# Two fused transformer blocks on one core: the second block opened with diagonal products and a channel-major first chunk

## The chip, the cores and the metric

One Trainium2 (trn2) chip, one of its cores. The metric is the device time of one execution of the whole program in microseconds (us), median of the runs shown; smaller is better. Engines are TensorE (PE in the profile; PEld is its weight load), VectorE (DVE), ScalarE (ACT), GpSimd (POOL) and SyncE (SP, which here only issues DMA transfers).

## What is computed

Batch 1, 512 tokens, width 1024, float32 in and out. The first block is attention plus a short convolution, then 16 experts of which each takes its 64 best tokens; the second block follows on its output.

```python
# end of block 1 (16 experts, 64 tokens each)
ye = (silu(xe @ w_gate) * (xe @ w_up)) @ w_down * gate     # per expert
x  = x + g2 * scatter_add(ye)                              # "combine"
x  = rmsnorm(x, final_norm_g)                              # output of block 1

# block 2
h = rmsnorm(x, norm_g)
u, v, za, ab, ab_gate, zb, g_a, g_b = split(h @ w_in + b_in)
y_a = gelu(u) * spatial_mix(layernorm(gelu(v))) * silu(za)
y_b = silu(groupnorm(conv31(ab * sigmoid(ab_gate)))) * silu(zb)
x = x + (sigmoid(g_a) * (y_a @ w_pa) + sigmoid(g_b) * (y_b @ w_pb)) @ w_out
x = x + sigmoid(rmsnorm(x, ple_norm_g) @ w_ple_gate) * (p @ w_ple)
out = rmsnorm(x, final_g)
```

The two normalisations at the seam meet on the same row: with a = 1/rms of block 1's output row before its gain, and e = the factor that both norms make together, the kernel works with one row `acc` (the sum after the last expert), the gain row `fng` (final_norm_g), and two numbers a row, `ae`.

## The kernel before, in words

Tokens lie in four tiles of 128 (`NT = 4`), channels in eight of 128 (`KT = 8`). Every large product of block 2 is made in three passes: both operands are split into a rounded part ("h") and a rest ("l"), and h*h, h*l and l*h are added up in PSUM (`mm3`). A weight chunk is 1024 x 256; `Weights.load` lets SP fetch it into a raw tile `wr` (two buffers), `Weights.steps` gives eight small steps per chunk that split it (ACT rounds into `wh`, L250; DVE subtracts into `wl`, L248), and the chunk that TensorE works on carries the steps of the next chunk along (`ahead`). The order on each engine is the order of the program's lines; nothing reorders it.

**Experts** (loop `for p in range(8)`, two experts a turn, on the two halves of TensorE's columns): `pair_gemm` with the gate weights into `pa_`, with the up weights into `pu`, with the down weights into `py`. Weights come as 1 MiB tiles `ew` through `eload`: each tile that has been used gives its buffer to the next tile in line. In turn p the sums of turn p-1 are put back to the tokens (`combine_half`, one-hot rows `GT` times `ybuf`, added to `acc` by DVE, L1261). The last turn (p = 7) loads its down weights in smaller pieces, column half n = 0 first, then n = 1, into one `py` tile of two banks; the four combines of half 0 stand in one place, before the third quarter of half 1.

**Gain rows.** `spread` makes a row in all 128 partitions out of a column: DVE writes the column on four diagonals (L900), TensorE multiplies with a matrix of ones (L903), ACT copies out (L904), twice a row. Turn 5 makes two rows so (`fng`, and `gg`, the product of both gains), turn 7 one (`b_in` of the v part).

**Opening of block 2.** The half-1 sum `ylast` is made by DVE (L1378); four combines (L1257) add it. For each token tile DVE multiplies by `gg` into `hr` (`h2_gain`, partly on POOL), ACT squares `acc` with a running sum (L1291), DVE weighs the squares with the squared gain (`x2_sums`, L1295), DVE and POOL make the two factors (`x2_stats`, L1453, L1454, and `power`, L179), ACT scales the row (L1465), TensorE turns it around in eight 128 x 128 transposes (`put_T`, L1427), ACT and DVE write `h2` as h and l (L1429, L1430). TensorE's first chunk is v chunk 0, token-major (`v_chunk(0)`): its four token tiles can start as soon as their own `h2` columns are there. After it stand `POOL` transfers and, on POOL, the multiplication of `acc` by `fng` (`xf_gain`, L1547); then four times a channel-major chunk for `ab_gate` and one for `ab`, and v chunks 1 to 3. From the first `ab` chunk on, DVE works off 31 convolution taps per channel tile in the background (L1593).

Of the kernel before, what the change touches and what calls it, by code (L numbers as in the profile page):

```python
# [62 lines left out]
def tile_two_blocks(ctx: ExitStack, tc: tile.TileContext, a, out):  # L63
# [373 lines left out]
    ci = [0]  # L437
# [458 lines left out]
    def spread(dst, cols_, tmp_):  # L896

        for n in range(2):
            d_ = tmp_()
            DVE.tensor_mul(d_.rearrange("p (a b) -> p a b", b=128), ident[:, None, :].to_broadcast([128, 4, 128]),  # L900
                           cols_[:, 4 * n:4 * n + 4, None].to_broadcast([128, 4, 128]))
            p_ = bank()
            PE.matmul(p_, one, d_, start=True, stop=True)  # L903
            ACT.activation(dst[:, n * 512:n * 512 + 512], p_, AF.Copy)  # L904

# [387 lines left out]
    def x2_sums(t, n):

        DVE.tensor_tensor_reduce(sqx[t], sqx[t], rows2[:, 0, half(n)], 1.0, sq4[:, t, 0, 1:2] if n else 0.0,  # L1295
                                 op0=OP.mult, op1=OP.add, accum_out=sq4[:, t, n, 1:2])

    for p in range(8):
# [60 lines left out]
        i0 += 16  # L1359
        ybuf[p] = big("yb", [2, D], F32R)  # L1360
        for n in range(2):
            for q, (k0, nk) in enumerate(lasts[n]):
                if n and q == 2:
                    x2_half(0, 0, tmp)
                    for t in range(NT):
                        if t < NT - 1:
                            x2_half(t + 1, 0, tmp)
                        x2_sums(t, 0)
                tiles = [etiles[i0 + e][0] for e in range(2)]
                i0 += 2  # L1370
# [25 lines left out]
    w2 = a["w_in_2"][0]  # L1396
    U0, V0, ZA0, AB0, AG0, ZB0, GA0, GB0 = (i * D for i in range(8))
    specs = [(w2, V0)]
    for j in range(4):
        specs += [(w2, AG0 + 256 * j), (w2, AB0 + 256 * j)]  # L1400
    specs += [(w2, V0 + 256 * j) for j in range(1, 4)]
    for j in range(4):
        specs += [(w2, U0 + 256 * j), (w2, ZA0 + 256 * j)]
    for j in range(4):
        specs += [(w2, GA0 + 256 * j), (a["w_pa_2"][0], 256 * j)]
    specs += [(w2, GB0 + 256 * j) for j in range(4)]
    specs += [(w2, ZB0 + 256 * j) for j in range(4)]
    specs += [(a["w_pb_2"][0], 256 * j) for j in range(4)]
    for n in ("w_out_2", "w_ple_gate_2"):
        specs += [(a[n][0], 256 * j) + (("mx",) if j % 2 else ()) for j in range(4)]  # L1410
    W = Weights(specs, {"mx": lambda sh: (big3("wxh", sh, F32R), big("wxl", sh, F32R))})
    ci[0] = 0
    lead[0] = 1
    W.load(1)
    gg = cst3[:, 0:D]
    cmat = identr
    strip = gp.tile([128, 128], F32R, name="strip", tag="post")
    rsel = strip[0:64, 96:104]
    bvb = rows2[:, 1]

    def put_T(dst, t, row):

        for n in range(2):
            p_ = bank("pT", (4, 128))
            for i in range(4):
                c = n * 512 + i * 128
                PE.transpose(p_[:, i], row[:, c:c + 128], ident)  # L1427
            ts = slice(t * 128, t * 128 + 128)
            ACT.activation(dst.h[n][:, :, ts], p_, AF.Copy)  # L1429
            DVE.tensor_sub(dst.l[n][:, :, ts], p_, dst.h[n][:, :, ts].bitcast(F32))  # L1430
# [26 lines left out]
    hrs = [big3("hr", [D]) for t in range(NT)]

    def h2_gain(t, n, eng=DVE):
        eng.tensor_tensor(hrs[t][:, half(n)], arow(t, half(n)), gg[:, half(n)], op=OP.mult)  # L1460

    def h2_row(t):
        for n in range(2):
            r = hrs[t][:, half(n)]
            ACT.activation(r, r, AF.Copy, scale=ae[:, t, 1:2])  # L1465

    def xf_row(t):
        ACT.activation(arow(t), arow(t), AF.Copy, scale=ae[:, t, 0:1])

    w0 = W.steps(0, lo_engine=POOL)  # L1470

    def w0_do(*js):
        for j in js:
            w0[j]()
# [446 lines left out]
```

## Time and profile before

| | |
|---|---|
| median of 3 runs | 1718.19 us (1715.05 to 1718.56) |
| the profiled execution, its own time | 1718.02 us |
| its span in the profile | 1716.3 us |
| TensorE busy | 1669.9 us, 97% of the span |
| DVE / ACT / POOL busy | 54% / 34% / 4% |

The profile is read from the outside in: the shares by engine say that TensorE is nearly always at work; the table by stretches says where it is not; the timeline of a stretch says what it waits for there. "Busy" counts an instruction's time at either clock, so the column PEclk, the granted share of TensorE's full clock (1.00 is 2.4 GHz, 0.50 is 1.2 GHz), is to be read beside it. A product on fp32 operands shows as two records.

### The profile page before, as it was taken

The page shows a single profiled execution, that of the slowest core. Times are in us where ns is not written, and L with a number is a line of the kernel's source. Part 1 is how long each engine was busy: PE and PEld are TensorE (multiplying, and loading weights), DVE is VectorE, ACT ScalarE, POOL GpSimd, SP SyncE. Part 2 cuts the span into 40 slices and gives each one's busy share as a digit, 9 for nine tenths or more (in the row PEclk, how much of TensorE's full clock was granted, in tenths as well). Part 3 has the DMA queues.
Part 4 walks back from the last instruction along what each step waited for, and adds up shares of the span by engine and source line. Part 5 has one row for each costly group of instructions (what it writes and reads, how often), then busy time and mean ns, then how long its engine had stood idle before and what let it go on. Part 6 is the DMA issues. An engine that isn't in the chain of part 4 may idle for free.

```text
span 1716.3 us, 22506 instructions
## 1 busy us (share of the span) xinstructions
PE 1669.9 (97%) x9212; PEld 1204.1 (70%) x9212; DVE 933.4 (54%) x1697; ACT 585.8 (34%) x1117; POOL 65.9 (4%) x68
## 2 busy tenths in 40 slices
PE   8999999989999999999999999979999999999998
PEld 5987787767888984444444344348898888877898
DVE  4667776565663442212121221286889999955544
ACT  5454444455222331111011011043335443354333
POOL 2000000000000000000000000050000000000000
PEclk9999999999999999999999999999999999999999
DMA  9132322202553769999999999833323233233421
GB/s 364 56 123 74 123 74 99 74 25 75 172 181 113 304 256 345 360 399 419 419 418 420 419 420 418 315 100 99 97 76 98 74 98 99 79 118 99 144 102 50
DMA packets 168028, 334.55 MB, mean 195 GB/s; under 512 B 6927, under 2 KB 103988, under 8 KB 167668
## 3 DMA queue, kind: packets, MB, share of 16 engines
q1 hardware_dynamic: 165520, 328.50, 51.6%
q0 software_dynamic: 1024, 2.37, 0.4%
q10 hardware_dynamic: 1380, 2.23, 0.4%
q8 instruction: 72, 1.18, 0.3%
q14 instruction: 32, 0.26, 0.0%
HBM read 328.89 MB, written 4.19 MB: 194 GB/s over the span
## 4 chain that ended last, share of the span: by engine, by line
PE 90%; DVE 6%; ACT 2%; issue 1%; DMA 1%; SPq 0%; POOL 0%; POOLq 0%; DVEq 0%; ACTq 0%
PE pb L289 16%; PE pb L290 15%; PE pb L291 15%; PE pu L1238 6%; PE py L1238 6%; PE pg L1202 4%; PE po L831 2%; PE pT L823 2%; PE s L792 1%; PE pg L1259 1%; PE pv L291 1%; PE py L1373 1%; PE pa__6640 L1238 1%; PE pa__6106 L1238 1%; PE pa__5837 L1238 1%
## 5 line engine op out<-in xcount | busy, mean ns | idle before, releaser
L248 DVE TENSOR_TENSOR wl<-wr,wh 128x512 fp32r<-128x512 f32 x316 | 225.2, 731 | 95.0 <-ACT wh L250 95.0
L250 ACT ACTIVATE wh<-wr 128x512 fp32r<-128x512 f32 x320 | 183.0, 620 | 78.8 <-PE pb L290 47.1
L1593 DVE SCALAR_TENSOR_TENSOR co<-cin,cols,co 128x512 f32<-128x512 f32 x240 | 188.3, 785 | 4.1
L289 PE MATMUL pb<-h2h,wh 128*128 128x512 f32 x448 | 177.4, 396 | 0.0
L290 PE MATMUL pb<-h2l,wh 128*128 128x512 f32 x448 | 174.9, 390 | 0.0
L291 PE MATMUL pb<-h2h,wl 128*128 128x512 f32 x448 | 174.8, 390 | 0.0
L289 PE MATMUL pb<-hxh,wh 128*128 128x512 f32 x320 | 130.5, 408 | 0.0
L290 PE MATMUL pb<-hxl,wh 128*128 128x512 f32 x320 | 125.3, 391 | 0.0
L291 PE MATMUL pb<-hxh,wl 128*128 128x512 f32 x320 | 125.2, 391 | 0.0
L1238 PE MATMUL pu<-ew,xe 128*64 128x512 f32 x512 | 114.8, 596 | 0.0
L1238 PE MATMUL py<-ew,hb 128*64 128x512 f32 x440 | 101.0, 597 | 0.0
L289 PEld LDWEIGHTS pb<-h2h,wh 128*128 128x128 f32 x448 | 84.5, 189 | 19.7 <-issue 2.4
L291 PEld LDWEIGHTS pb<-h2h,wl 128*128 128x128 f32 x448 | 84.3, 188 | 17.8
L290 PEld LDWEIGHTS pb<-h2l,wh 128*128 128x128 f32 x448 | 84.3, 188 | 17.2 <-issue 0.5
L1273 DVE SCALAR_TENSOR_TENSOR yt<-py,gt__5834,g2b 128x512 f32<-128x512 f32 x15 | 10.6, 747 | 144.7 <-PE py L1238 138.3
L1238 PEld LDWEIGHTS pu<-ew,xe 128*64 128x64 f32 x512 | 35.4, 137 | 66.0 <-issue 62.9
L802 ACT ACTIVATE P<-P,m 128x512 f32<-128x512 f32 (+1 forms) x64 | 49.7, 777 | 85.8 <-DVE m L801 83.2
L798 DVE CUSTOM_DVE_ANT_0 P<-s,cst,sink 128x512 f32<-128x512 f32 (+1 forms) x64 | 52.2, 815 | 46.2 <-PE s L795 45.9
L1205 ACT ACTIVATE xe<-pg,modc,ga 128x128 f32<-128x128 f32 x64 | 25.8, 453 | 146.2 <-PE pg L1202 146.2
L1202 PEld LDWEIGHTS pg<-Gs,xr 128*128 128x128 f32 x512 | 59.5, 192 | 21.5 <-issue 19.5
L291 PEld LDWEIGHTS pb<-hxh,wl 128*128 128x128 f32 x320 | 60.2, 188 | 13.5
L289 PEld LDWEIGHTS pb<-hxh,wh 128*128 128x128 f32 x320 | 60.3, 188 | 11.4 <-issue 2.3
(468 smaller groups left out, 3305.8 us busy)
## 6 DMA issues: line engine op xcount, KB each, us to landing
ew<-w_exp_gate SPq DMA_DIRECT2D x64, 1024.0 KB, 14.2
ew<-w_exp_up SPq DMA_DIRECT2D x64, 1024.0 KB, 13.9
ew<-w_exp_down SPq DMA_DIRECT2D x59, 1024.0 KB, 14.7
wr<-w_in SPq DMA_DIRECT2D x58, 1024.0 KB, 5.6
wr<-w_mod SPq DMA_DIRECT2D x16, 1024.0 KB, 5.1
wm<-w_mod SPq DMA_DIRECT2D x8, 1024.0 KB, 11.8
wr<-w_out SPq DMA_DIRECT2D x8, 1024.0 KB, 4.9
wr<-w_proj_attn SPq DMA_DIRECT2D x4, 1024.0 KB, 5.1
```

The lines of the kernel that those rows point to most:

```text
L248: (lo_engine or DVE).tensor_tensor(lo[:, ks], raw[:, ks], hi[:, ks].bitcast(F32), op=OP.subtract)
L250: ACT.activation(hi[:, ks], raw[:, ks], AF.Copy)
L289: PE.matmul(ps, ah, bh, start=first, stop=False)
L290: PE.matmul(ps, ah, bl, start=False, stop=False)
L291: PE.matmul(ps, al, bh, start=False, stop=last)
L798: DVE.tensor_tensor_reduce(p_[:, :n], s2[:, self.s0:self.s0 + n], self.mask, 1.0, sink8[:, 4 * g + i:4 * g + i + 1], op0=OP.add, op1=OP.ma ...
L802: ACT.activation(p_[:, :n], p_[:, :n], AF.Exp, bias=m4[:, i:i + 1], scale=0.125, accum_out=sm[:, i:i + 1])
L823: PE.transpose(p_[:, i, :], self.P[i][:, kk * 128:kk * 128 + 128], ident)
L831: PE.matmul(po[64 * h:64 * h + 64], V[:, vi, g * 64:g * 64 + 64], last[:, :, h, :], start=(kk == 1), stop=(kk == nk), tile_position=(0, 64 ...
L1202: PE.matmul(p_[:, d], xrow(t, ds), Gs[p][:, t], start=(t == 0), stop=(t == NT - 1))
L1238: PE.matmul(ps[64 * e:64 * e + 64, n], lhs(k, e), tiles[e][kk][:, n * 512:n * 512 + 512], start=(k == 0), stop=(k == KT - 1), tile_positio ...
L1593: DVE.scalar_tensor_tensor(co[ct], cin[ct][:, k:k + 512], ctap(k, ct), co[ct], op0=OP.mult, op1=OP.add)
```

## The change

It rewrites the seam between the blocks.

- `fng` is fetched from memory by one broadcast transfer on ACT's queue in turn 5; the row of `b_in` likewise, on POOL's queue, beside the spatial weights; `spread`, the row `gg` and the squared gain go.
- The last 14 expert tiles don't take the `wr` buffers, and the first two weight chunks of block 2 are loaded into them before the last down weights are multiplied (`W.load(1)`).
- Half 1 of the last down product gets a PSUM tile of its own (`py1`); the combines of half 0 stand in two places, two token tiles each.
- `x2_half` multiplies by `fng` on DVE into a second row `xf` (`xrow2`) and lets ACT square both rows; `xf_gain` on POOL and `x2_sums` go, and later stages read `xrow2`.
- The four combines of half 1 now stand ahead of everything else. Then, instead of scaling rows and transposing, TensorE multiplies each 128 x 128 block of `xf` with a diagonal matrix `dg` of the row factors (`h2_T`), which scales and turns in one product; the gain `norm_g` comes in as a scale per partition when ACT and DVE write `h2` (`h2_put`).
- The first chunk is the `ab_gate` chunk 0, channel-major (`first_chunk`): step k uses channel tile k of all tokens, both column halves; channel tiles 6 and 7 of `h2` are made inside it. v chunk 0 moves to the other v chunks, after the `ab` chunks; the spatial mask, transposes and biases move from `ab` chunk 0 to `ab` chunk 1.

```diff
-            if i < len(elist):
+            if i < len(elist) and not (tag == "wr" and i >= len(elist) - 14):
...
     def x2_half(t, n, tile_):
         combine_half(7, t, n)
-        x2_square(t, n, tile_)
+        DVE.tensor_mul(xrow2(t, half(n)), arow(t, half(n)), fng[:, half(n)])
+        for i, row in enumerate((arow, xrow2)):
+            ACT.activation(tile_("sqx"), row(t, half(n)), AF.Square, scale=D ** -0.5,
+                           accum_out=sq4[:, t, n, i:i + 1])
...
-            g12 = small("g12", 8)
-            spread(fng, column("final_norm_g", 0, 8), tmp)
-            DVE.tensor_mul(g12, column("final_norm_g", 0, 8), column("norm_g_2", 0, 8))
-            spread(cst3[:, 0:D], g12, tmp)
+            ACT.dma_start(out=fng, in_=brow("final_norm_g", 0, D))
...
+        W.load(1)
+        py = [py[:, 0], bank3("py1")[:, 0]]
...
                 if n and q == 2:
-                    x2_half(0, 0, tmp)
-                    for t in range(NT):
-                        if t < NT - 1:
-                            x2_half(t + 1, 0, tmp)
-                        x2_sums(t, 0)
+                    for t in range(2):
+                        x2_half(t, 0, tmp)
+                if n and q == 3:
+                    for t in range(2, NT):
+                        x2_half(t, 0, tmp)
...
+    def x2_diag(t):
+        DVE.tensor_scalar(dg[:, t], ident, ae[:, t, 1:2], None, op0=OP.mult)
...
+    def h2_T(t, k):
+        if not t:
+            hT[k] = bank("hT", (NT, 128))
+        PE.matmul(hT[k][:, t], xrow2(t, slice(k * 128, k * 128 + 128)), dg[:, t], start=True, stop=True)
+
+    def h2_put(k):
+        p_ = hT.pop(k).rearrange("p a b -> p (a b)")
+        g_ = column("norm_g_2", k)
+        ACT.activation(h2.hi(k), p_, AF.Copy, scale=g_)
+        DVE.scalar_tensor_tensor(h2.lo(k), p_, g_, h2.hi(k).bitcast(F32), op0=OP.mult, op1=OP.subtract)
+
+    K0 = 6
+    for t in range(NT):
+        x2_half(t, 1, lambda name: jk)
+        if t:
+            x2_stats(t - 1)
+        if t > 1:
+            x2_diag(t - 2)
+    for t in range(2):
+        for k in range(K0):
+            h2_T(t, k)
+    x2_stats(NT - 1)
+    x2_diag(NT - 2)
+    for k in range(K0):
+        h2_T(NT - 2, k)
+    w0_do(2)
+    x2_diag(NT - 1)
+    for k in range(K0):
+        h2_T(NT - 1, k)
+        h2_put(k)
+        if k in (1, 3):
+            w0_do(2)
...
-    def xf_gain():
-        for t in range(NT):
-            POOL.tensor_tensor(arow(t), arow(t), fng, op=OP.mult)
...
-    for j in range(1, 4):
+    for j in range(4):
         run_bg(v_chunk(j), 0.5)
```

TensorE in the up stage of turn 7, before (`pa__`, `pu`: gate and up sums; L903 is the product of `spread`):

```order
L1238 MATMUL pa__7728<-ew,xe 64x512 x8
L1238 MATMUL pu<-ew,xe 64x512 x8
L903 MATMUL pb<-t,one 128x512 x2
L1238 MATMUL pu<-ew,xe 64x512 x8
L1212 MATMUL pg<-aff,Gu 128x2 x4
```

The same place in the changed kernel:

```order
L1228 MATMUL pa__7707<-ew,xe 64x512 x8
L1228 MATMUL pu<-ew,xe 64x512 x16
L1202 MATMUL pg<-aff,Gu 128x2 x4
L1228 MATMUL pu<-ew,xe 64x512 x8
L1214 MATMUL pg<-cst,Gu 128x128 x4
```

The two products of `spread` are gone from between the up products; in turn 5 four go.

TensorE from the last combine of half 0 into the opening, before (L1373 the down products, L1257 the combines of half 1, L1427 transposes, L289 to L291 v chunk 0):

```order
L1259 MATMUL pg<-yb,GT 128x512
L1260 MATMUL pg<-yb,GT 128x512
L1373 MATMUL py<-ew,hb 64x512 x8
L1257 MATMUL pg<-hb,GT 128x512 x4
L1427 MATMUL pT<-cst,hr 128x128 x8
L289 MATMUL pv<-wh,h2h_7985 128x256
L290 MATMUL pv<-wl,h2h_7985 128x256
L291 MATMUL pv<-wh,h2l_7987 128x256
```

And in the changed kernel (L1457 the diagonal products, L1499 the first chunk):

```order
L1249 MATMUL pg<-yb,GT 128x512
L1250 MATMUL pg<-yb,GT 128x512
L1385 MATMUL py_7866<-ew,hb 64x512 x4
L1247 MATMUL pg<-hb,GT 128x512 x4
L1457 MATMUL hT<-dg,xf_7867 128x128 x12
L1457 MATMUL hT<-dg,xf_7868 128x128 x12
L1499 MATMUL pb<-h2h_8008,wh 128x512 x2
L1499 MATMUL pb<-h2h_8008,wl 128x512 x2
L1499 MATMUL pb<-h2l_8010,wh 128x512 x2
```

Before, the first transposes stand right behind the combines and each token tile's products behind its own transposes; now all 24 diagonal products of channel tiles 0 to 5 come first, and the first chunk after them.

DVE at the opening, before (L1378 makes `ylast`, L1261 the sums, L1460 the gain, L1295 the weighed squares, L1453 and L1454 the factors):

```order
L1378 SCALAR_TENSOR_TENSOR hb<-py,gt__5834,g2b 128x512
L1460 TENSOR_TENSOR hr<-acc_6119,cst_7348 128x512 x2
L1261 TENSOR_TENSOR acc_6119<-pg,acc_6119 128x512 x2
L1460 TENSOR_TENSOR hr<-acc_6119,cst_7348 128x512
L1295 ISA sqx,sq_5836<-sqx,rows_7813,sq_5836 128x512
L1295 ISA sq_5836 128x1
L1453 SCALAR_TENSOR_TENSOR ae<-sq_5836 128x1
L1454 SCALAR_TENSOR_TENSOR ae<-ae,sq_5836 128x1
```

And in the changed kernel, from the multiplication of token tile 0 to the first diagonal matrix (L1251 the sums, L1280 the gain, L1435 to L1437 the factors, L1441 the diagonal):

```order
L1280 TENSOR_TENSOR xf_7867<-acc_6119,fng 128x512
L1251 TENSOR_TENSOR acc_6119<-pg,acc_6119 128x512
L1280 TENSOR_TENSOR xf_7867<-acc_6119,fng 128x512
L1435 SCALAR_TENSOR_TENSOR ae<-sq_5836 128x1
L1436 TENSOR_TENSOR ae<-sq_5836 128x1
L1437 SCALAR_TENSOR_TENSOR ae<-ae 128x1
L1251 TENSOR_TENSOR acc_6120<-pg,acc_6120 128x512
L1280 TENSOR_TENSOR xf_7868<-acc_6120,fng 128x512
L1435 SCALAR_TENSOR_TENSOR ae<-sq_5836 128x1
L1436 TENSOR_TENSOR ae<-sq_5836 128x1
L1437 SCALAR_TENSOR_TENSOR ae<-ae 128x1
L1441 TENSOR_SCALAR dg<-cst,ae 128x128
```

Sum, gain and factors of the tiles go in turn, and the diagonal of tile 0 stands behind the factors of tile 1.

## Rows read from the trace of the kernel before

**Rows 1.** The page: its head, and the chain of work that ended last, by engine.

```profile
span 1716.3 us, 22506 instructions
...
PE 90%; DVE 6%; ACT 2%; issue 1%; DMA 1%; SPq 0%; POOL 0%; POOLq 0%; DVEq 0%; ACTq 0%
```

**Rows 2.** Busy time by stretches: the stretch and its length (us), busy time and instructions of PE, PEld, DVE, ACT, POOL, then the granted TensorE clock, the mean busy share of the DMA engines, and GB/s.

```profile
730.00:1085.00 355.00, 348.85 (x1759) 153.11 (x1756) 71.07 (x119) 42.10 (x88) 0.00 (x0) 1.00 1.02 417
...
1106.00:1108.00 2.00, 1.15 (x8) 0.42 (x4) 1.22 (x2) 0.00 (x0) 0.00 (x0) 1.00 0.18 71
...
1131.50:1136.40 4.90, 1.27 (x8) 0.84 (x8) 4.83 (x12) 3.51 (x8) 2.63 (x3) 1.00 0.00 0
1136.40:1143.30 6.90, 4.35 (x19) 4.06 (x20) 6.87 (x12) 3.59 (x8) 5.47 (x5) 0.51 0.00 0
...
1157.60:1163.70 6.10, 6.05 (x25) 5.85 (x26) 3.22 (x6) 0.86 (x2) 0.00 (x0) 0.50 0.27 61
...
1400.00:1490.00 90.00, 90.00 (x398) 74.12 (x397) 88.37 (x123) 30.27 (x54) 9.64 (x6) 1.00 0.29 89
```

**Rows 3.** Timeline of PE, experts: start (us), length, engine, line, operation, count, and in brackets the idle time before and what ended it. `pa__` opens turns 5, 6 and 7; L1202 is the gather of the next turn's tokens.

```profile
947.36 1.03 PE L1238 MATMUL pa__7172<-ew,xe 128*64 128x512 f32 x4
...
982.30 2.05 PE L1202 MATMUL pg<-Gs,xr 128*128 128x128 f32 x16
...
987.39 3.93 PE L903 MATMUL pb<-t,one 128*128 128x512 f32 x8 [1.47 <-DVE t L900]
...
1011.17 3.60 PE L1238 MATMUL pa__7462<-ew,xe 128*64 128x512 f32 x16
...
1069.59 0.60 PE L1238 MATMUL pa__7728<-ew,xe 128*64 128x512 f32 x2
```

**Rows 4.** Timeline of PE, the end of turn 7 (same columns).

```profile
1092.37 1.98 PE L903 MATMUL pb<-t,one 128*128 128x512 f32 x4
1094.28 3.65 PE L1238 MATMUL pu<-ew,xe 128*64 128x512 f32 x16
...
1103.02 3.65 PE L1238 MATMUL pu<-ew,xe 128*64 128x512 f32 x16
...
1116.81 3.65 PE L1373 MATMUL py<-ew,hb 128*64 128x512 f32 x16 [0.85 <-DVE yt L1273]
...
1123.16 3.65 PE L1373 MATMUL py<-ew,hb 128*64 128x512 f32 x16
1127.67 3.70 PE L1257 MATMUL pg<-hb,GT 128*128 128x512 f32 x8 [0.85 <-DVE hb L1378]
```

**Rows 5.** Timeline of SP's queue, 1060 to 1220 us: first issue, time over which the issues go out, their count; and of the page's DMA issues one row with the median time from issue to landing (us) last.

```profile
1073.68 29.21 SPq L1068 DMA_DIRECT2D ew<-w_exp_down  x12
1118.77 97.03 SPq L210 DMA_DIRECT2D wr<-w_in  x9
...
ew<-w_exp_down SPq DMA_DIRECT2D x59, 1024.0 KB, 14.7
```

**Rows 6.** Timeline of PE, opening of block 2 and the chunks behind it: 1134.81 the first transposes, 1157.65 the last part of v chunk 0, 1162.51 `ab_gate` chunk 0, 1174.01 `ab` chunk 0, 1253.88 v chunk 1, 1289.36 the chunk behind v chunk 3.

```profile
1134.81 1.27 PE L1427 MATMUL pT<-cst,hr 128*128 128x128 f32 x8 [3.44 <-ACT hr L1465]
...
1157.65 0.58 PE L291 MATMUL pv<-wh,h2l 128*128 128x256 f32 x1 [4.03 <-DVE h2l L1430]
...
1162.51 0.63 PE L289 MATMUL pb<-h2h,wh 128*128 128x512 f32 x1
1162.93 0.63 PE L290 MATMUL pb<-h2l,wh 128*128 128x512 f32 x1
...
1174.01 0.39 PE L289 MATMUL pb<-h2h,wh 128*128 128x512 f32 x1
1174.24 0.39 PE L290 MATMUL pb<-h2l,wh 128*128 128x512 f32 x1
...
1253.88 0.28 PE L289 MATMUL pv<-wh,h2h 128*128 128x256 f32 x1
...
1289.36 0.40 PE L289 MATMUL pb<-h2h,wh 128*128 128x512 f32 x1
```

**Rows 7.** Timeline of DVE in the opening.

```profile
1129.98 1.27 DVE L1261 TENSOR_TENSOR acc<-pg,acc 128x512 f32<-128x512 f32 x2
...
1132.45 0.15 DVE L1453 SCALAR_TENSOR_TENSOR ae<-sq 128x1 f32<-128x1 f32 x1
...
1133.31 0.68 DVE L1460 TENSOR_TENSOR hr<-acc,cst 128x512 f32<-128x512 f32 x1
...
1140.21 1.43 DVE L1460 TENSOR_TENSOR hr<-acc,cst 128x512 f32<-128x512 f32 x1
...
1148.04 8.95 DVE L248 TENSOR_TENSOR wl<-wr,wh 128x512 fp32r<-128x512 f32 x2
...
1164.81 0.21 DVE L1575 TENSOR_SCALAR strip<-cst 128x128 fp32r<-128x128 f32 x1
```

**Rows 8.** Timeline of POOL and of ACT in the opening.

```profile
1132.87 0.70 POOL L179 TENSOR_TENSOR ae<-ae,mhalf 128x2 f32<-128x2 f32 x1 [3.36 <-DVE ae L1454]
...
1139.81 2.96 POOL L248 TENSOR_TENSOR wl<-wr,wh 128x512 fp32r<-128x512 f32 x2
...
1146.42 9.41 POOL L1547 TENSOR_TENSOR acc<-acc,fng 128x1024 f32<-128x1024 f32 x4
...
1130.69 0.63 ACT L1291 ACTIVATE sqx<-acc 128x512 f32<-128x512 f32 x1 [3.68 <-DVE acc L1261]
```

More of the change, by code (lines that the diff above doesn't have):

```diff
@@ L894, in tile_two_blocks @@
     DVE.memset(one, 1.0)
[L896 to L904, printed above, removed]
     def gate_start(tag, off):
@@ L1359, in tile_two_blocks @@
         i0 += 16
+        W.load(1)
+        py = [py[:, 0], bank3("py1")[:, 0]]
+        xf.extend(big(f"xf{i}", [2, D]) for i in range(2))
+        strip = gp.tile([128, 128], F32R, name="strip", tag="post")
+        rsel = strip[0:64, 96:104]
+        DVE.tensor_scalar(strip, ident, 0.0, None, op0=OP.mult)
+        for z in range(2):
+            DVE.tensor_scalar(strip[:, 31 + 32 * z:32 + 32 * z], ident[:, 0:1], 0.0, 1.0 / 128, op0=OP.mult, op1=OP.add)
+        DVE.tensor_add(rsel, ident[0:64, 0:8], ident[0:64, 32:40])
+        DVE.tensor_scalar(cmat, ident, -1.0 / 128, None, op0=OP.add)
         ybuf[p] = big("yb", [2, D], F32R)
@@ L1377, in tile_two_blocks @@
                 ylast = hb[:, 0, half(1)]
-                DVE.scalar_tensor_tensor(ylast, py[:, 1], gt_[:, p:p + 1], g2b[:, half(1)], op0=OP.mult, op1=OP.mult)
+                DVE.scalar_tensor_tensor(ylast, py[1], gt_[:, p:p + 1], g2b[:, half(1)], op0=OP.mult, op1=OP.mult)
             else:
@@ L1394, in tm @@
         return tq.tile([128] + list(shape), F32, name=name, tag="t")
[L1396 to L1430, printed above, removed]
+    bvb = cst3[:, 0:D]
     st = gp.tile([128, NT, 4, 6], F32, name="st")
@@ L1455, in x2_stats @@
         power(ae[:, t])
[L1457 to L1465, printed above, removed]
-    def xf_row(t):
[L1468 to L1474, printed above, removed]
@@ new lines, in first_chunk @@
+    def first_chunk(post):
+        i, (wh, wl) = 0, W.parts[0]
+        ci[0] = 1
+        ps = [bank() for m in range(2)]
+        nxt = W.steps(1)
+        for k in range(KT):
+            if k == 6:
+                W.parts.pop(0)
+            for z, (w_, x_) in enumerate(((wh, h2.hi), (wl, h2.hi), (wh, h2.lo))):
+                for m in range(2):
+                    PE.matmul(ps[m], w_[:, k, m * 128:m * 128 + 128], x_(k), start=(k == 0 and z == 0),
+                              stop=(k == KT - 1 and z == 2))
+            if k in (1, 2):
+                for t in range(NT):
+                    h2_T(t, k + 5)
+                h2_put(k + 5)
+            if k == 3:
+                w0_do(2)
+            if k > 3:
+                for f in nxt[:2]:
+                    f()
+                nxt = nxt[2:]
+        for m in range(2):
+            post(m, ps[m])
@@ L1633, in post_ab @@
             conv_bg(ct)
-        run_bg(ct_chunk(h2, post_g, bhooks[j][0]), 0.55)
+        if j:
+            run_bg(ct_chunk(h2, post_g, bhooks[j][0]), 0.55)
+        else:
+            spatial_load()
+            first_chunk(post_g)
+            pvar = bank("pvar", (512,))
         run_bg(ct_chunk(h2, post_ab, bhooks[j][1]), 0.55)
-    for j in range(1, 4):
+    for j in range(4):
         run_bg(v_chunk(j), 0.5)
```

130 lines of the change are left out of this document (52 added, 78 removed).

## Prediction, made before the changed kernel ran

> **What bounds the kernel now.** The chain of waits comes first: 90% of it is TensorE [rows 1]. So the question is where TensorE is not working, or works slowly, and whether the change touches it. The table by stretches gives the places. In the expert stage TensorE is busy 348.85 of 355 us at full clock, while the transfers run at 417 GB/s without a pause [rows 2]: two resources, both nearly full. In the conv stage later (1400 to 1490 us) TensorE is busy 90.00 of 90 us and VectorE 88.37 [rows 2]. Between them lies the seam. From 1131.5 to 1136.4 us TensorE works 1.27 us; from 1136.4 to 1143.3 the granted clock is 0.51, and again 0.50 from 1157.6 to 1163.7 [rows 2]. The timeline names the two long waits: 3.44 us for ScalarE's first scaled row, and 4.03 us for VectorE's last `h2l` [rows 6]. That last wait is not VectorE's own work: two `wl` subtractions take 8.95 us, where a like operation on two SBUF tiles takes 0.68 [rows 7], while GpSimd spends 9.41 us on the four multiplications of `xf_gain`, from 1146.42 [rows 8].
>
> **A yardstick.** I compare both kernels where v chunk 0 and `ab_gate` chunk 0 are both done, since the change swaps their order. Before, that is at 1174.01 us, where `ab` chunk 0 starts [rows 6]. In the changed kernel `ab` chunk 0 comes after `ab_gate` chunk 0 alone, and v chunk 0 is owed. Its price at full clock: v chunks 1 to 3 run from 1253.88 to 1289.36 [rows 6], with four group-norm products among them at 0.23 each (1174.24 less 1174.01 [rows 6]); (35.48 - 0.9) / 3 = 11.5 us.
>
> **What comes earlier, up to the first combine of half 1.**
> - *Turn 5 without `spread`.* Turn 5 takes 1011.17 - 947.36 = 63.81 us, turn 6 takes 1069.59 - 1011.17 = 58.42 [rows 3]; the difference, 5.39, is the four products of 3.93 and the 1.47 wait ahead of them [rows 3]. All of it lies on TensorE's path: -5.4.
> - *Turn 7 without `spread`.* 1094.28 - 1092.37 = 1.91 [rows 4]: -1.9.
> - *`py1`.* The 0.85 us that half 1 waits for `yt` to read the shared tile [rows 4] goes: -0.85.
> - *Combines of half 0 in two places.* Four now take 2.77 us (1120.39 to 1123.16) [rows 4], with a VectorE sum awaited in between. Split, that wait hides; but VectorE now also multiplies by `fng`, so it reaches `ylast` some 0.3 us after TensorE's last down product. I put the two at zero; together they can be 0.5 either way.
> - *`fng` by transfer.* 0.5 MiB on queues that carry 417 GB/s [rows 2] is 1.3 us of transfer time. It hides behind the lead of the expert tiles. That lead: the last up tile was issued before the first down tile, at 1073.68 [rows 5]; with a median of 14.7 us to landing [rows 5] it is there by about 1088.4, and used from 1103.02 [rows 4]: 14.6 us. TensorE's 7.3 us and the transfer's 1.3 leave 6. The later turns do not refill it: a turn's 25.2 MB at 417 GB/s is 60.3 us against TensorE's 58.4, which is why the spare time matters at all.
> - *`wr` buffers withheld.* The last eight (half-size) tiles wait for the release of a tile two steps later, some 4 us. The transfers run dry at about 1106 us [rows 2], and the last tiles are used after 1123.16 [rows 4]; 17 us of cover, less 7.3 and less 4, is enough. In return the first weights of block 2, issued at 1118.77 before [rows 5], are there ahead of the seam.
>
> Sum: 5.4 + 1.9 + 0.85 = 8.15, so the combines of half 1 start at 1127.67 - 8.15 = 1119.5 [rows 4].
>
> **The opening, counted from that start.** TensorE's four combines take 3.7 us [rows 4]. VectorE can add tile 0 at 1.1. Its sums and multiplications go at about 0.65 each (1.27 for two, 0.68 alone) and a factor needs three small operations at 0.15 to 0.17 [rows 7]. The queue puts the first diagonal behind three sums, three multiplications and six small ones: 1.1 + 6 x 0.65 + 6 x 0.17 + 0.21 = 6.2. ScalarE's squares at 0.63 and GpSimd's power at 0.70 [rows 8] fit beside that. So TensorE idles from 3.7 to 6.3, **2.6 us**.
>
> A diagonal product is an fp32 product of 128 x 128 with new weights each time, which the gather does already: 16 records, 8 products, in 1.89 us from row to row (2.05 as given) [rows 3], so 0.24 each. The bounds: 0.16, the transposes that go (1.27 for eight, a wait inside [rows 6]), and 0.48, twice 0.24, if the clock is at half. I take 0.24, the same shape. Six for tile 0 end at 7.75; tile 1's diagonal follows one more tile's work (0.65 x 2 + 0.5 + 0.2) at 8.3; six end at 9.8, the next twelve at 12.7, their diagonals being ready at 9.1 and 10.0.
>
> The first chunk has 48 products at 0.227 (10.9 us) and the eight late diagonal products (1.9): 25.5. VectorE's rests of `h2` and of the weights, twelve at 0.7, start at about 9.1 and end by 20; step 7 needs its own only at 24. For some eight hand-overs between engines I add 1.0: **X = 26.5**. Its bounds: 24.5 without hand-overs and with cheap products, 29.5 with the products at half clock.
>
> **The sum.** New yardstick: 1119.5 + 26.5 + 11.5 = 1157.5, against 1174.0: **-16.5 us**. Behind it I count nothing. v chunk 0 gets convolution taps beside it, where v chunks 1 to 3 already carry theirs. The spatial mask and biases, about 3.5 us of VectorE, meet taps in `ab` chunk 1; VectorE then lags TensorE, but the weight splits are issued half a chunk (5.5 us) ahead, and the later stretch still has 1.6 us to spare in 90 [rows 2]. If that cover were gone, TensorE would wait for `wl`, at most those 3.5 us.
>
> The profiled execution took 1718.02 us, 1.7 over its span and 0.17 under the median of 1718.19. So 1718.19 - 16.5 = **1701.7 us**.
>
> **Rivals.**
> - *A. The clock falls once more.* TensorE's idle time is 2.6 us, then a short burst and 0.6. Before, 0.85 us stalls [rows 4] left the clock at full; a wait of 3.44 and the wait of 4.03 [rows 6] were each followed by a stretch of 6 to 7 us at 1.2 GHz [rows 2]. 2.6 lies between. Half of 6.5 us is 3.2, less the 0.6 gap that then hides: +2.6, 1704.3. Chance 0.25.
> - *B. Transfers bound the experts.* 60.3 us a turn against 58.4 speaks for it; the lead of 14.6 against it. If the lead were already spent, the 7.3 us of the two `spread`s would turn into waits for tiles: 1709.0. Chance 0.09.
> - *C. GpSimd holds VectorE up.* One of VectorE's multiplications, at 1133.31, ran 0.68 us although it began while GpSimd's power (1132.87, 0.70) was on [rows 7, 8]; another, at 1140.21 beside a GpSimd subtraction, took 1.43 [rows 7, 8]. If each of the four powers cost VectorE its own 0.70, the chain of diagonals would be 2.8 us longer: 1704.5. The Trainium skill, page "SBUF — State Buffer", section "SBUF: two separate sides", has such a rule: of a VectorE operation with two SBUF inputs and a GpSimd operation that reads SBUF, whichever starts first locks a shared pair of ports for its whole length and the other stands still. By that rule these 2.8 us would be paid; the 8.95 us row agrees with it, the 0.68 us row does not. Chance 0.11.
> - *D. The lower clock stays.* In 1.2 GHz the chunk's products go at 0.42 (1162.93 less 1162.51 [rows 6]) instead of 0.227. If the opening kept TensorE too patchy for the clock to return, each us there would lose a half. The gain is eaten from 33 us at low clock on; through the first chunk and the next (about 40 us) it would be 1721.7, slower than before. Against: both stretches before ended after 6 to 7 us, once work was dense [rows 2]. Chance 0.03.
>
> **How the numbers follow.** The forecast itself, 1701.7 with its own range of 1699 to 1704, has 0.52. A to D have 0.25, 0.09, 0.11 and 0.03. About 0.2% (3.4 us) is what a measurement can tell from no change here: all cases but D are faster by more; B together with A and C would come to 1714.4, near that limit, so I give 0.03 to no change and 0.03 to slower, 0.94 to faster. The range goes down to 1697.5 (X at 24.5 gives 1699.7; one of the three runs lay 3 us under the median, so 2 more) and up to 1709.5, which takes in B.
>
> **What would show it.** Right: turn 5 as long as turn 6; no 0.85 us wait before half 1; one idle stretch of 2 to 3 us behind the combines of half 1, then diagonal products at 0.24; `ab` chunk 0 starting about 26.5 us after the first of these combines; VectorE's `wl` subtractions at 0.7; the clock at full throughout (or once low, case A). Wrong: TensorE waiting for `ew` tiles in turn 7 (B), sums or multiplications on VectorE over 1 us beside L179 (C), more than one stretch at 0.50 (D), or TensorE waiting for `wl` between `ab` chunk 1 and the v chunks.

## Result, and the profile after

The changed kernel took 1704.28 us (median; 1703.84 to 1706.10), the one before 1718.31 in the same comparison: ratio **0.9925, interval 0.9907 to 0.9942**, 14.0 us less. A second comparison (experiment 2) gave 0.9934 (0.9921 to 0.9946). The forecast was 16.5 us less, and its range holds both medians. The profiled execution took 1703.84 us, 1.7 over its span.

The page of the changed kernel, its head and the chain by engine [rows 1]:

```profile
span 1702.1 us, 22530 instructions
...
PE 89%; DVE 5%; DMA 2%; ACT 1%; issue 1%; SPq 1%; POOL 0%; POOLq 0%; DVEq 0%; ACTq 0%
```

DMA has gone from 1 to 2%: more of the path than before now waits for transfers. TensorE's timeline in the changed kernel (columns as in [rows 3, 4, 6]): turns 5, 6 and 7, the last down products, the opening, `ab` chunk 0, and last the chunk behind v chunk 3.

```profile
948.79 1.46 PE L1228 MATMUL pa__7172<-ew,xe 128*64 128x512 f32 x6
...
1007.20 1.03 PE L1228 MATMUL pa__7441<-ew,xe 128*64 128x512 f32 x4
...
1065.58 1.46 PE L1228 MATMUL pa__7707<-ew,xe 128*64 128x512 f32 x6
...
1102.83 4.50 PE L1385 MATMUL py<-ew,hb 128*64 128x512 f32 x18
1107.75 7.32 PE L1385 MATMUL py<-ew,hb 128*64 128x512 f32 x30 [0.42 <-DMA ew<-w_exp_down]
1115.00 0.50 PE L1249 MATMUL pg<-yb,GT 128*128 128x512 f32 x1
...
1122.22 3.70 PE L1247 MATMUL pg<-hb,GT 128*128 128x512 f32 x8 [1.17 <-DVE hb L1390]
1128.71 1.58 PE L1457 MATMUL hT<-dg,xf 128*128 128x128 f32 x12 [2.78 <-DVE dg L1441]
1130.47 4.29 PE L1457 MATMUL hT<-dg,xf 128*128 128x128 f32 x36 [0.19 <-DVE dg L1441]
1134.51 0.71 PE L1499 MATMUL pb<-h2h,wh 128*128 128x512 f32 x2
...
1147.32 0.39 PE L289 MATMUL pb<-h2h,wh 128*128 128x512 f32 x1
...
1274.17 0.40 PE L289 MATMUL pb<-h2h,wh 128*128 128x512 f32 x1
```

Read it in four stretches, against [rows 3, 4, 6] of before:

| stretch (us) | before | after | difference | forecast |
|---|---|---|---|---|
| start to turn 5 | 947.36 | 948.79 | +1.43 | 0 |
| turn 5 to the first combine of half 1 | 180.31 | 173.43 | -6.88 | -8.15 |
| from there to the end of v chunk 3 | 161.69 | 151.95 | -9.74 | -8.35 |
| the rest | 426.9 | 427.9 | +1.0 | 0 |

The part that I summed came out at -16.62, against -16.5, but only because one stretch fell short by 1.3 us and the next gained 1.4; 2.4 us were lost where I had counted nothing, and a wait for an expert tile had come into the second stretch. Its 0.42 us is the smaller part of its price. The 24 down products up to the next combine (48 records: half 0 and the first half of half 1) run in pairs on the two halves of the array, the starts of a pair 7 ns apart. Here they fall out of step: the two records ahead of the wait stand alone, and so do the last two. They take 1115.00 - 1102.83 = 12.17 us, against 10.45 without the wait (experiment 9).

VectorE, then GpSimd, in the changed kernel's opening [rows 7, 8]:

```profile
1121.42 0.74 DVE L1390 SCALAR_TENSOR_TENSOR hb<-py,gt__5834,g2b 128x512 f32<-128x512 f32 x1
...
1126.38 0.68 DVE L1251 TENSOR_TENSOR acc<-pg,acc 128x512 f32<-128x512 f32 x1
1127.10 0.69 DVE L1280 TENSOR_TENSOR xf<-acc,fng 128x512 f32<-128x512 f32 x1
...
1128.27 0.29 DVE L1441 TENSOR_SCALAR dg<-cst,ae 128x128 f32<-128x128 f32 x1
...
1131.28 0.69 DVE L248 TENSOR_TENSOR wl<-wr,wh 128x512 fp32r<-128x512 f32 x1
```

```profile
1126.55 0.70 POOL L179 TENSOR_TENSOR ae<-ae,mhalf 128x2 f32<-128x2 f32 x1 [491.52 <-DVE ae L1437]
1128.21 0.70 POOL L179 TENSOR_TENSOR ae<-ae,mhalf 128x2 f32<-128x2 f32 x1 [0.96 <-DVE ae L1437]
...
1131.19 0.70 POOL L179 TENSOR_TENSOR ae<-ae,mhalf 128x2 f32<-128x2 f32 x1 [0.20 <-DVE ae L1437]
```

VectorE's product at 1127.10, which begins while GpSimd's power of 1126.55 is on, and its subtraction at 1131.28 beside the power of 1131.19 take 0.69 each, both from two SBUF tiles: no sign of case C.

The transfers show where to look. Busy time by stretches (columns as in [rows 2]) of the changed kernel:

```profile
10.00:40.00 30.00, 29.51 (x209) 20.56 (x207) 15.52 (x34) 16.43 (x30) 6.27 (x10) 0.94 1.09 353
780.00:830.00 50.00, 49.22 (x258) 22.42 (x256) 7.54 (x13) 5.39 (x12) 0.00 (x0) 1.00 1.03 409
1100.00:1110.00 10.00, 8.64 (x42) 2.99 (x40) 2.53 (x8) 0.60 (x1) 0.00 (x0) 1.00 1.05 387
```

and of the kernel before, in the two stretches where both programs do the same work:

```profile
10.00:40.00 30.00, 29.43 (x213) 20.79 (x212) 15.56 (x34) 16.54 (x30) 6.80 (x11) 0.94 1.08 388
780.00:830.00 50.00, 49.22 (x257) 22.48 (x256) 7.54 (x13) 5.39 (x12) 0.00 (x0) 1.00 1.03 419
```

The engines' columns agree; only the last differs, 409 GB/s against 419, and 353 against 388 in the first 40 us. The 387 GB/s between 1100 and 1110 us, where before was running dry [rows 2], is no sign of it: experiment 9 has 386 there at the full rate.

### The profile page after: what moved, and what is told of

Same layout as the page of the kernel before. It is cut to its first block, busy times and chain, and to the rows that moved or that the text cites. A ratio compares the mean times of both kernels' runs of the same rounds, so it can differ in the third digit from the quotient of the medians.

```text
span 1702.1 us, 22530 instructions
## 1 busy us (share of the span) xinstructions
PE 1663.1 (98%) x9232; PEld 1201.1 (71%) x9232; DVE 916.5 (54%) x1687; ACT 582.5 (34%) x1118; POOL 49.4 (3%) x59
## 4 chain that ended last, share of the span: by engine, by line
PE 89%; DVE 5%; DMA 2%; ACT 1%; issue 1%; SPq 1%; POOL 0%; POOLq 0%; DVEq 0%; ACTq 0%
PE pb L289 15%; PE pb L290 15%; PE pb L291 15%; PE py L1228 6%; PE pu L1228 6%; PE pg L1192 4%; PE po L831 2%; PE pT L823 2%; PE s L792 1%; PE pg L1249 1%; PE pv L291 1%; PE pv L289 1%; PE pv L290 1%; PE pa__7441 L1228 1%; PE pa__5837 L1228 1%; PE pa__6906 L1228 1%
## 5 line engine op out<-in xcount | busy, mean ns | idle before, releaser
L248 DVE TENSOR_TENSOR wl<-wr,wh 128x512 fp32r<-128x512 f32 x320 | 216.9, 697 | 98.9 <-ACT wh L250 98.7
L289 PE MATMUL pb<-h2h,wh 128*128 128x512 f32 x432 | 170.8, 395 | 0.0
L291 PE MATMUL pb<-h2h,wl 128*128 128x512 f32 x432 | 168.3, 390 | 0.0
L290 PE MATMUL pb<-h2l,wh 128*128 128x512 f32 x432 | 168.2, 389 | 0.0
L289 PE MATMUL pb<-hxh,wh 128*128 128x512 f32 x320 | 130.1, 406 | 0.0
L291 PE MATMUL pb<-hxh,wl 128*128 128x512 f32 x320 | 125.3, 391 | 0.0
L289 PEld LDWEIGHTS pb<-h2h,wh 128*128 128x128 f32 x432 | 81.1, 188 | 19.0 <-issue 2.4
L291 PEld LDWEIGHTS pb<-h2h,wl 128*128 128x128 f32 x432 | 81.1, 188 | 17.2
L291 PEld LDWEIGHTS pb<-hxh,wl 128*128 128x128 f32 x320 | 60.0, 188 | 13.2
L289 PEld LDWEIGHTS pb<-hxh,wh 128*128 128x128 f32 x320 | 60.2, 188 | 11.5 <-issue 2.3
```

Of the source, the lines that this page charges most:

```text
L248: (lo_engine or DVE).tensor_tensor(lo[:, ks], raw[:, ks], hi[:, ks].bitcast(F32), op=OP.subtract)
L289: PE.matmul(ps, ah, bh, start=first, stop=False)
L290: PE.matmul(ps, ah, bl, start=False, stop=False)
L291: PE.matmul(ps, al, bh, start=False, stop=last)
```

## Experiments

Two questions: why are transfers slower in stretches that the diff doesn't touch, and what is each part worth? On the first the theories were: the chip or the run (theory 1 of experiments 1 and 2), the change itself (theory 2), then a row fetched on ScalarE's queue, and at last the place of the buffers in SBUF.

**1 and 2. Both kernels again, with profiles from one chip.** No edit.

> The kernel before once more, with a profile of its own on the chip that the next three run on. Two theories on why TensorE waited for an expert tile in turn 7 of the changed kernel. Theory 1 (the rate): the expert transfers run at 409 GB/s there against 419 in the profile of before, in stretches whose program is the same, so the rate belongs to the chip or the run; then this profile shows the same rate as the changed kernel in this call, whichever it is, and its last tiles land later than 1103.9 us if the rate is 409. Theory 2 (the change): the changed kernel itself lowers the rate; then this profile shows 417 to 420 and the changed kernel 409. Time 1715 to 1719 us either way.

> The changed kernel once more. Theory 1 (the rate belongs to the chip or the run): expert transfers at the rate of the kernel before in this call; with 417 to 420 GB/s no wait for an expert tile in the last down products and the first combine of half 1 about 1.4 us sooner against the start of turn 5; with 409 the wait of 0.42 us again. Theory 2 (the change lowers the rate): 409 again beside 419. Ratio to before 0.991 to 0.993 in both; by theory 1 at 419, 0.990 to 0.992.

Before: 1718.45 us, ratio 1.0002 (0.9993 to 1.0011), 419 GB/s at 780 to 830 us. After: 1706.17 us, 0.9934 (0.9921 to 0.9946), 409 GB/s, a wait of 0.50 us for a down tile. The run and the chip are out: the rate goes with the program.

**3. The rows alone.**

```diff
-            spread(fng, column("final_norm_g", 0, 8), tmp)
-            DVE.tensor_mul(g12, column("final_norm_g", 0, 8), column("norm_g_2", 0, 8))
-            spread(cst3[:, 0:D], g12, tmp)
+            ACT.dma_start(out=fng, in_=brow("final_norm_g", 0, D))
+            ACT.dma_start(out=cst3[:, 0:D], in_=brow("norm_g_2", 0, D))
...
-            side[1] = lambda: spread(rows2[:, 1], column("b_in_2", 8, 8), tmp)
+            ACT.dma_start(out=rows2[:, 1], in_=brow("b_in_2", D, D))
```

(`g12` is gone, and the gains are multiplied on VectorE in turn 7.)

> The kernel before with its three rows (fng, the gains, the bias) fetched by broadcast and no products for them; the opening of block 2 stays as it was. My terms: 5.4 us in turn 5 and 1.9 in turn 7 come off TensorE's path and nothing comes back, so 7.3 us less: ratio 0.9957 (0.9950 to 0.9965). Rival (the transfers take over): turns 5 and 7 get shorter but TensorE waits for expert tiles in turn 7 or its last down products, and half or more of the 7.3 returns: 0.998 to 1.000.

1717.16 us, ratio 0.9996 (0.9987 to 1.0005), as the rival had it. TensorE, turn 7 of this kernel:

```profile
1090.09 3.65 PE L1238 MATMUL pu<-ew,xe 128*64 128x512 f32 x14 [0.59 <-DMA ew<-w_exp_up]
...
1101.61 3.65 PE L1238 MATMUL pu<-ew,xe 128*64 128x512 f32 x14 [1.17 <-DMA ew<-w_exp_up]
...
1112.45 2.80 PE L1372 MATMUL py<-ew,hb 128*64 128x512 f32 x12 [0.50 <-DMA ew<-w_exp_down]
```

From turn 5 to the first combine of half 1 only 0.61 us of the 7.3 is left (1127.81 - 948.11 = 179.70 us, against 180.31). The three waits for tiles are 2.26 us; the rest went into products that run slower around them and into a turn 6 of 59.27 us, where it was 58.42. The transfers ran at 409 GB/s.

**4. `xf_gain` on VectorE, in the kernel before.**

```diff
-            POOL.tensor_tensor(arow(t), arow(t), fng, op=OP.mult)
+            DVE.tensor_tensor(arow(t), arow(t), fng, op=OP.mult)
```

> The kernel before with the four multiplications by fng (xf_gain) on VectorE in place of GpSimd; all else as before. Theory (GpSimd's use of SBUF holds VectorE up): the two wl subtractions fall from 8.95 us to 1.4, the wait of 4.03 us ahead of v chunk 0's h2l products goes, and the second stretch at half clock with it (3.4 us more); VectorE pays 5.5 us in the second ab_gate chunk, of which up to 2 may show: 5 to 7.4 us less, ratio 0.9957 to 0.9971. Rival (VectorE was slow for another reason, the queue order or the landing of the weights): wl stays slow or the wait moves, ratio 0.999 to 1.001.

1711.92 us, ratio 0.9963 (0.9950 to 0.9975), as the theory had it. VectorE in that opening:

```profile
1149.91 0.68 DVE L248 TENSOR_TENSOR wl<-wr,wh 128x512 fp32r<-128x512 f32 x1
1151.05 0.69 DVE L248 TENSOR_TENSOR wl<-wr,wh 128x512 fp32r<-128x512 f32 x1 [0.45 <-ACT wh L250]
```

0.68 and 0.69 us, where the pair took 8.95 [rows 7]; the wait of 4.03 us [rows 6] and the second stretch at half clock are gone. So 6 us, of the 9.7 that the new opening gave, could be had by moving four multiplications from GpSimd to VectorE, without any diagonal. The Trainium skill's rule on the shared pair of ports (page "SBUF — State Buffer", section "SBUF: two separate sides"), by which the operation that starts first holds the other up until it ends, agrees with these rows. It does not show beside GpSimd's 128 x 2 powers above, where VectorE's operations on two SBUF tiles keep their 0.69 us.

**5 to 7. Which fetch lowers the rate?** In the changed kernel, `fng` on GpSimd's queue (5); in the kernel before, the late row `ple_norm_g_2` on ScalarE's queue (6); the rows alone, on GpSimd's queue (7; the edit of experiment 3 with `POOL` for `ACT`, not shown):

```diff
-            ACT.dma_start(out=fng, in_=brow("final_norm_g", 0, D))
+            POOL.dma_start(out=fng, in_=brow("final_norm_g", 0, D))
...
-    plg = brows("g1b", "ple_norm_g_2")
+    plg = brows("g1b", "ple_norm_g_2", q=ACT)
```

> The changed kernel with fng fetched on GpSimd's queue in place of ScalarE's. So far the expert transfers ran at 409 GB/s in the three profiles of programs with a broadcast fetch on ScalarE's queue, and at 419 in the three without, from the first microseconds on and whatever the run. Theory 1 (that queue): 419 here, no wait for an expert tile in the last down products, about 1.5 us less there and up to 1 us less at the start: ratio 0.990 to 0.992. Theory 2 (any added fetch of a row, on whatever queue, or the run): 409 again, the wait of 0.4 to 0.5 us again, ratio 0.9925 to 0.9935.

> The kernel before, with one row that it fetches near its end (ple_norm_g_2, for the last stage) fetched on ScalarE's queue in place of GpSimd's; nothing is fetched more than before. Theory 1 (a broadcast fetch on ScalarE's queue makes the whole program's transfers slower): 409 GB/s in the expert stage, 350 and not 386 in the first 40 us, though the fetch itself comes after 1500 us; time within 3 us of before. Theory 2 (the traffic of the fetch itself, or more bytes): 419 as before.

> The kernel before with its three rows fetched by broadcast as in the run of the rows alone, but on GpSimd's queue. By theory 1 on the rate (ScalarE's queue): 419 GB/s, the lead of the expert tiles suffices, TensorE waits for none in turn 7, and the 7.3 us of the products with ones show in full, less what 1.5 MB at 419 GB/s takes from the lead: ratio 0.9955 to 0.9965. By theory 2 (any fetch, or the transfers bound the experts in any case): 0.999 to 1.000 as in the run on ScalarE's queue, with the same waits.

5: 1703.93 us, 0.9921 (0.9908 to 0.9935), 409 GB/s and a wait of 0.49. 6: 1717.67 us, 1.0001 (0.9992 to 1.0010), 418 GB/s. 7: 1713.75 us, 0.9980 (0.9971 to 0.9989), 409 GB/s, one wait of 0.45. As the cause of the rate, ScalarE's queue has fallen on both sides: 409 without it, 418 with it. The time of 7 met neither forecast (0.9955 to 0.9965, 0.999 to 1.000): at the same 409 GB/s it is 3.4 us under experiment 3, with one wait where that had three. The queue seems to matter to the waits, though not to the rate; how, no run shows.

**8. The opening alone:** the changed kernel with `spread` back in turn 5, for `fng` and the bias, and no fetch for either (its definition comes back too, not shown).

```diff
-            ACT.dma_start(out=fng, in_=brow("final_norm_g", 0, D))
+            spread(fng, column("final_norm_g", 0, 8), tmp)
+            spread(cst3[:, 0:D], column("b_in_2", 8, 8), tmp)
...
-        POOL.dma_start(out=bvb, in_=brow("b_in_2", V0, D))
```

> The changed kernel with both rows (fng and the bias) made by the products with ones again, in turn 5 as before the change, and no broadcast fetch for them. Turn 5 is 63.8 us again; all that is left of the change is the opening, py1, the combines in two places and turn 7 without products with ones. My terms: 16.5 less 5.4 is 11.1 us under before: ratio 0.9935 (0.993 to 0.994), with transfers at 419 GB/s and no wait for an expert tile. Rival (the opening alone is worth the whole of the change's 12 to 14 us because the rows gave nothing back): 0.992 to 0.9925.

1706.01 us, 0.9938 (0.9924 to 0.9951), as the forecast of 0.9935 had it; no wait for a tile. But 409 GB/s where 419 was forecast, with neither row fetched. So it is not the fetches that lower the rate. What this program shares with the other slow ones is that `g12` is gone: two buffers of 32 bytes per partition in the first SBUF pool. In the built programs every buffer behind that pool lies 64 bytes lower; the lowest expert buffer begins at byte 28352 of a partition, where it began at 28416 = 111 x 256.

**9. The 64 bytes given back**, in the changed kernel.

```diff
+            pad = small("pad", 8)
+            DVE.memset(pad, 0.0)
             ACT.dma_start(out=fng, in_=brow("final_norm_g", 0, D))
```

> The changed kernel with 64 bytes per partition given back to its first SBUF pool, by one small tile (two buffers of eight floats) that nothing reads. Background: all programs at 409 GB/s so far lack the small tile g12, which the change dropped with the products that made the gains; one of them has no broadcast fetch at all, so theory 1 on ScalarE's queue has fallen. With g12 gone every later buffer lies 64 bytes lower: the first expert buffer at 28352 in place of 28416, which is 111 times 256. Theory 3 (the place of the buffers): with the tile back, transfers at 419 GB/s, 386 in the first 40 us, no wait for an expert tile in turn 7, 1.5 to 2.9 us less there and some 0.7 to 1.4 less ahead of turn 5: ratio 0.9900 to 0.9920 (the changed kernel itself 0.9925 to 0.9934). Theory 4 (the rate depends on something else in the program, its size for one): 409 GB/s and 0.9925 to 0.9940.

1701.30 us, ratio **0.9902 (0.9888 to 0.9915)**, as theory 3 had it. Stretches of this kernel:

```profile
10.00:40.00 30.00, 29.45 (x211) 20.57 (x210) 15.65 (x35) 16.62 (x30) 6.39 (x11) 0.94 1.08 388
780.00:830.00 50.00, 49.22 (x256) 22.30 (x254) 7.55 (x13) 5.40 (x12) 0.00 (x0) 1.00 1.03 419
...
1126.68:1130.09 3.41, 3.41 (x19) 3.41 (x18) 2.81 (x12) 1.97 (x5) 1.75 (x3) 0.50 0.00 0
```

and its TensorE:

```profile
1102.18 10.52 PE L1387 MATMUL py<-ew,hb 128*64 128x512 f32 x48
1112.63 0.50 PE L1249 MATMUL pg<-yb,GT 128*128 128x512 f32 x1
...
1126.34 7.22 PE L1459 MATMUL hT<-dg,xf 128*128 128x128 f32 x48 [2.78 <-DVE dg L1443]
1133.32 0.71 PE L1501 MATMUL pb<-h2h,wh 128*128 128x512 f32 x2
```

388 and 419 GB/s are back, no tile is waited for, and the 24 down products (48 records) take 10.45 us in place of 12.17. The last two rows are case A: after the same wait of 2.78 us the granted clock is 0.50 (1.2 GHz) for 3.41 us, and the 24 diagonal products (48 records) take 6.98 us, where the changed kernel took 5.80.

**10. The opposite:** the kernel before, with one buffer of `g12` in place of two, and no instruction changed.

```diff
-            g12 = small("g12", 8)
+            g12 = cp.tile([128, 8], F32, name="g12", tag="g12", bufs=1)
```

> The kernel before with one buffer of g12 in place of two: no instruction differs, every buffer behind the first pool lies 32 bytes lower. Theory 3 (the place of the buffers): 409 GB/s in the expert stage and about 350 in the first 40 us; the time 0 to 2.5 us longer, since the expert tiles' lead still covers a lower rate there: ratio 1.000 to 1.0015. Theory 4 (something else): 419 GB/s as before.

1718.61 us, 1.0004 (0.9995 to 1.0013), and in its stretches:

```profile
10.00:40.00 30.00, 29.45 (x213) 20.74 (x211) 16.01 (x35) 16.98 (x30) 6.27 (x10) 0.94 1.09 353
780.00:830.00 50.00, 49.22 (x258) 22.41 (x256) 7.54 (x13) 5.40 (x12) 0.00 (x0) 1.00 1.03 409
```

32 bytes lower costs the same 10 GB/s. The time does not show it: from turn 5 to the first combine of half 1 it is 180.29 us, against 180.31, so with the `spread` products in turns 5 and 7 the tiles' lead still covers the lower rate.

**11. The rows alone, with the 64 bytes back** (experiments 3 and 9 together).

> The kernel before with its three rows fetched by broadcast (on ScalarE's queue, as in the first run of the rows alone) and the 64 bytes given back. Theory 3: 419 GB/s, no or one short wait for an expert tile in turn 7, and the 7.3 us of the products with ones show nearly in full: ratio 0.9955 to 0.997, where the same rows without the 64 bytes gave 0.9996. Rival (the lead is too small for 7.3 us at any rate): 0.998 to 1.000, with waits for expert tiles at 419 GB/s.

1709.82 us, ratio 0.9954 (0.9941 to 0.9968), where experiment 3 had 0.9996. Turn 5 to the first combine of half 1 is 7.50 us shorter than before, against 7.3 forecast; in that kernel's last down products the only wait is the old one for `yt`:

```profile
1100.99 7.09 PE L1374 MATMUL py<-ew,hb 128*64 128x512 f32 x32
1108.93 3.65 PE L1374 MATMUL py<-ew,hb 128*64 128x512 f32 x16 [0.85 <-DVE yt L1273]
```

**12. The wait filled:** experiment 9 and two products that nothing reads.

```diff
+    fill = bank("fill", (512,))
+    for i in range(2):
+        PE.matmul(fill, ident, fng[:, half(i)], start=True, stop=True)
     h2 = Split("h2", 512)
```

> The changed kernel with the 64 bytes given back and two more products of 128 x 128 by 512, whose result nothing reads, between the combines of half 1 and the first diagonal product. Of the profiles of the changed opening so far, two had the clock fall once there, for 3.4 us, and two not, with the same wait of 2.78 us; where it fell the 24 diagonal products took 1.2 us longer. Theory (the wait is at the edge of what lets the clock fall): with TensorE busy for some 1.8 of the 2.78 us the clock stays at full, the diagonal products take 5.8 us, and the time is that of the run with the 64 bytes alone or up to 1.2 us less. Rival (the added products delay the first diagonal one): up to 1 us more.

1699.44 us, ratio **0.9891 (0.9878 to 0.9905)**, the fastest version here. TensorE:

```profile
1122.28 1.88 PE L1476 MATMUL fill<-fng,cst 128*128 128x512 f32 x4
1125.23 1.58 PE L1459 MATMUL hT<-dg,xf 128*128 128x128 f32 x12 [1.07 <-DVE dg L1443]
1126.99 4.29 PE L1459 MATMUL hT<-dg,xf 128*128 128x128 f32 x36 [0.19 <-DVE dg L1443]
```

The clock stays at full from 1118 to 1300 us, and the diagonal products take 5.80 us, 1.2 less than in experiment 9. That the two products did it is not shown: this is one profile, and two of the five without them kept the clock too. The difference to experiment 9 in time, 1.9 us, is not larger than the two intervals, and in the profiles 1.1 us of it was there before turn 5 (947.03 us against 948.16).

## Why the prediction was right, point by point

- **Turn 5**: 1007.20 - 948.79 = 58.41, and turn 6 58.38. Right, to 0.01.
- **Turn 7, and the rows together**: 7.50 in experiment 11 against 7.3. Right, at 419 GB/s.
- **`py1`, combines in two places**: no wait before half 1's products. `ylast` is 0.32 late (1.17 against 0.85), as written; the combines lose their wait (2.25 against 2.77 us). Zero, within 0.5.
- **`fng` by transfer, 6 us of lead left**: the one step that failed. It rested on 417 GB/s, a rate that I took from before [rows 2] and held fixed. At 409 a turn's 25.2 MB take 61.6 us, at 419 60.1; over six turns that is by estimate 9 us, more than the 6 left. Hence the wait, 12.17 - 10.45 = 1.7 us: rival B in part, from a cause that I had not named. At 419 GB/s the wait is gone (experiment 9).
- **`wr` buffers withheld**: they are withheld in experiment 9 too, without a wait. Right.
- **The opening**: the wait 2.78 (2.6 forecast), the first diagonal product at 6.5 (6.3), 24 in 5.80 us, so 0.24 each. X was 1147.32 - 1122.22 = 25.1, against 26.5. The 24 products ended at 12.3, where I had 12.7, and the 1.0 us for hand-overs was not paid: 1134.51 to 1147.32 is 12.81 us, just 48 x 0.227 + 8 x 0.24.
- **Nothing behind it**: from `ab` chunk 0 to the end of v chunk 3 126.85 us, against 115.35 before plus 11.5. Right.
- **Case A**: the clock fell once in three of the five profiles with the wait of 2.78 or 2.79 us (experiments 2, 5, 9) and not in two (the changed kernel's first, experiment 8). It costs 1.2 us, not 2.6: the stretch at half clock was 3.41 us long, where I had taken the 6 to 7 of before.
- **Cases C and D**: not seen.
- **Ahead of turn 5**: +1.43 in the changed kernel. 1.0 of it is one wait. TensorE waits 1.61 us for VectorE's `xr`, where it waited 0.59, and VectorE for a transfer that the chain of the work that ended last gives 9.18 us, where it took 8.17. The chain's rows and TensorE's, before and then after:

```profile
572.87 8.17 DMA xr<-x
...
581.88 0.66 PE L1012 MATMUL pT<-cst,xr 128*128 128x128 f32 x4 [0.59 <-DVE xr L1004]
```

```profile
573.27 9.18 DMA xr<-x
...
583.29 0.65 PE L1002 MATMUL pT<-cst,xr 128*128 128x128 f32 x4 [1.61 <-DVE xr L994]
```

  The seven profiles at 409 GB/s reach turn 5 0.7 to 2.5 us after before, 1.3 on average; the six others at 418 or 419 from 0.7 sooner to 0.8 later, 0.0 on average. That goes with the rate, but not with it alone: near 31 us the granted clock is 0.50 for 3.4 us in some profiles of either rate and not in others, once in two profiles of the kernel before.
- **Behind v chunk 3**: +1.0, where I had counted nothing. TensorE's last product comes 419.5 us after the start of the chunk behind v chunk 3, against 419.4; the other 0.9 us is the landing of the last output transfer, 6.92 us after that product, against 6.06. It is the same 6.92 in experiment 2, but 6.13 in experiments 5 and 8, which have the same rate: why is open.

So the median came 2.6 us over the forecast. Within the sum, luck helped: the opening came 1.4 better and the experts 1.3 worse. What is left over lies outside the sum, 1.4 us ahead of turn 5 and 1.0 at the end. With the 64 bytes back the median is 1701.3, and the forecast was 1701.7; that, too, is partly luck, since there the clock fell, which cost the 1.2 us by which the opening was better, and turn 5 still began 0.8 us late.

## What to carry to other kernels

Before counting what an edit does, compare a long stretch that it doesn't touch in both profiles, and in a second profile of the kernel before: if its GB/s differ with the program, and not from profile to profile, the edit has moved something that the diff doesn't name. (780 to 830 us gave 419 in both profiles of the kernel before; 10 to 40 us gave 388 and 377, the clock 0.94 and 1.00.) Dropping a small tile from a pool moves all pools behind it, and a lead that is the difference of two nearly equal rates is gone with 2% of either. And where VectorE's simple operations take several times their usual length, as here 8.95 us for two of 0.68, look at what GpSimd does at that moment.

## What the hardware showed that I had not expected

Where the lowest expert buffer began at 28416, in seven profiles, the expert transfers ran at 418 or 419 GB/s; 64 bytes lower (six profiles) or 32 (one), at 409. The first weights (10 to 40 us) went at 388 and at 353 or 354; one profile of the kernel before had 377.

The two losses, 2.4% and 9%, are one. In the packet records of the traces a row of 4096 bytes of an expert tile takes 159 ns (median) in the faster programs and 164 in the slower; the first weights come in rows of 1024 bytes, which take 46 ns and 51. So a row of either length costs 5 ns more, and the shorter rows lose the larger share.

The Trainium skill, page "DMA: Bandwidth & Descriptors", section "How a descriptor splits into AXI transactions", has a rule of this kind: a transaction must start at a multiple of 256 bytes, so a descriptor that starts elsewhere also pays for the bytes from the multiple below. By it a row of 4096 bytes at 192 past the multiple would take 134 beats in place of 128, and one at 128 past it 132, estimates of 5% and 3% from that page. These traces agree only in direction. In the program of the kernel before, 10 of the 16 expert buffers in use from 740 to 1080 us begin at a multiple of 256 and 6 at 128 past one, and rows to either take the same 159 ns (81 and 54 tiles). In the slower programs the buffers begin 64 and 192 past a multiple, or 96 and 224, and rows to all of them take 164 ns. So what went with the loss here is a start that is no multiple of 128 bytes. That it is the start address itself is likely, not shown: no run shifted the buffers by a whole 128 or 256 bytes.
